# Differential attention on one core: score products with the second operand on 64 rows or on all 128

## The chip, the cores and the metric

The kernel runs on 1 core of one Trainium2 chip. The metric is the device time in microseconds of one execution. Three runs of the kernel before were timed.

## What is computed

A trunk of two decoder layers over 1024 tokens of width 1024, all in float32. Layer 0 mixes tokens by gated linear attention, layer 1 by differential attention; each mixer is followed by an MLP of width 4096 with a squared ReLU. The change lies in layer 1:

```python
def diff_mixer(h, cos, sin, w_in, lam_vecs, subln_g, w_o, lambda_init):
    H, dh, dv = DIFF_HEADS, DIFF_DH, DIFF_DV          # 8, 64, 128
    q, k, v = jnp.split(h @ w_in, 3, axis=-1)
    q = rope_partial(q.reshape(B, T, H, 2, dh), cos, sin) * (dh ** -0.5)
    k = rope_partial(k.reshape(B, T, H, 2, dh), cos, sin)
    ...
    for i in range(T // Q_BLOCK):                     # 8 query tiles of 128
        L = (i + 1) * Q_BLOCK
        s = jnp.einsum('bhiqd,bhikd->bhiqk', qb, k[:, :, :, :L]).astype(f32)
        p = jax.nn.softmax(jnp.where(mask, s, -jnp.inf), axis=-1)
        a = p[:, :, 0] - lam * p[:, :, 1]
        outs.append(jnp.einsum('bhqk,bhkv->bhqv', a.astype(v.dtype), v[:, :, :L]))
```

Each of the 8 heads has two softmaxes (s = 0, 1) with queries and keys of 64 dimensions of their own, and one set of values of 128 dimensions.

## The kernel before, in words

**Precision.** A float32 operand is cut into a rounded part hi and a rest lo = x - hi, both of type float32r. A product x·y is the sum hi·hi + hi·lo + lo·hi: three TensorE products (`mm3`, L115).

**Layer 1's order.** TensorE's instructions in this stage stand in an order written out by hand (L1054); those of ScalarE, VectorE and GpSimd are ordered by the framework's planner, and each engine works through its queue in order. Time is counted in slots. A slot issues one score block (L1062), the pieces that an `Agenda` has due (transpositions, values, norms), and between them pieces of the projections: three products of 384 columns each, 64 pieces to a head, about 2.67 pieces per slot. When the projections are through, pieces of the output projection (512 columns) take their place. The projections run ahead of the scores by 22 slots.

**Score blocks.** There are 192: for each head and softmax, query tile i (0 to 7) needs the keys 0 to 128(i+1). These come in blocks b of at most 512 columns: one block for i below 4 and two from i = 4 on. In the order of issue a head has 24 blocks: eight for tiles 0 to 3 (called its first part below), sixteen for tiles 4 to 7 (its second part). Block (i, s, b) is written as those three numbers. `scores` (L904) takes one of three PSUM buffers `ps_` and issues two products: L920 on all 128 rows, L921 on 64 rows. Then VectorE puts on the causal mask (L923) and takes the row maximum (L924); when the tile's last block has come, it makes the negative scaled maximum `nm`, and ScalarE takes the exponential (L936), which frees the buffer. After s = 1 VectorE forms the difference of the two softmaxes (L951).

**Operands of the scores.** `turn_qk` (L877) transposes rotated queries (gi = 0) or keys (gi = 2) of a head and a half of the tokens: 128 partitions, the 64 dimensions of s = 0 above those of s = 1. From that tile it makes, for each s:

- queries `q`: hi in the half of the partitions of s (ScalarE, L887), lo in the other half (VectorE, L889): [hi; lo];
- keys `kd`: hi in its own half (ScalarE, L896), copied to the other half by GpSimd (L900): [hi; hi]; and a tile `kl` with the lo parts of both s (VectorE, L898).

L920 multiplies [hi; lo] with [hi; hi]: hi·hi + lo·hi. L921 multiplies the hi half of the queries with the lo half of the keys, on 64 partitions: hi·lo.

**Behind the scores.** `turn_a` (L960) transposes the weights on TensorE (L966), ScalarE and VectorE cut them in two (L112, L113, tile `aT`), and `values` (L972) multiplies them with the values into `po`. `sub_rms` and `sub_norm` apply the head's norm. `rotate` (L863) is GpSimd's rotary embedding, six operations per head and half. In the last two heads VectorE and ScalarE also cut up the weights of the output projection and reloaded outputs (L1030), and add output products to x (L712).

Of the kernel before, what the change touches and what calls it, by code (L numbers as in the profile page):

```python
# [40 lines left out]

# How much other work of TensorE lies between a piece of work and one that needs its results: in
# rough microseconds of products (gated linear attention), in slots (differential attention).
GLA_LAG = dict(rank=1.09, decay=4.71, keys=3.36, score=4.04, out=7.24, step=2.16, turn=14.56, ada=30.5)
DIFF_LAG = dict(rotary=2.55, keys=1.95, turn=3, next=1.6, value=2, rms=2.66, norm=6.53)
DIFF_END = dict(turn=1.27, next=0.57, value=1.15, rms=1.1, norm=2)
DIFF_LEAD = 22
DIFF_RATE = {True: 2.0, False: 3.0}    # pieces of the output projection per slot, before and after its last operand


class Agenda:
    """Work that is put off until enough other work has been issued (`now` counts it)."""

# [16 lines left out]
def two_pi_parts():  # L70
    """2*pi cut into parts of four bits, so that a part times an integer below 2**20 is exact."""
    rest, parts = 2.0 * math.pi, []
    step = 2.0 ** -1
    while step > 2.0 ** -46:
        part = math.floor(rest / step) * step
        parts.append(part)
        rest -= part
        step /= 16.0
    return [p for p in parts if p]
# [3 lines left out]
def trunk(ctx: ExitStack, tc, a, out):  # L83
    nc = tc.nc
    pe, act, dve, pool = nc.tensor, nc.scalar, nc.vector, nc.gpsimd

# [1 line left out]
    const = ctx.enter_context(tc.tile_pool(name="const", bufs=1))  # L88
# [20 lines left out]

# [1 line left out]
    def split(hi, lo, src):  # L111
# [8 lines left out]
    def weight(src, shape, pinned=False):  # L120
        """Load a piece of a weight and split it into two parts of float32r."""
        raw = wraw.tile(shape, F32, name="raw", tag="raw")
        c0 = 0
        for part in src if isinstance(src, list) else [src]:
            c1 = c0 + part.shape[-1]
            i = nc.sync.dma_start(out=raw[:, :, c0:c1], in_=part)
            c0 = c1
            if pinned:
                in_order(i)
        hi = wsp.tile(shape, F32R, name="whi", tag="whi")  # L130
        lo = wsp.tile(shape, F32R, name="wlo", tag="wlo")
        split(hi, lo, raw)
        return hi, lo

    def wcols(w, c0, n, pinned=False):
        """Columns of a weight with its rows on partitions: [128, k, n]."""
        return weight(w.rearrange("(k p) n -> p k n", p=P)[:, :, c0:c0 + n], [P, KT, n], pinned)
# [9 lines left out]
    def rsqrt_cols(r, ms, scratch, n, scale=1.0 / D):  # L147
        """r = (ms * scale + eps) ** -0.5 for a few columns, with a Newton step."""
        m = scratch.tile([P, n], F32, name="rs_m", tag="rs_m")
# [9 lines left out]
    def broadcast(bc, cols, n):  # L159
        """bc[:, j*128:(j+1)*128] = cols[:, j] on every partition."""  # L160
        for j in range(n):
            pe.matmul(out=bc[:, j * P:(j + 1) * P], lhsT=cols[:, j:j + 1].broadcast_to([P, P]),  # L162
                      rhs=ident, start=True, stop=True)

    def norm_mod(x, half, h, gcols, shift, tmp, small, ps, cols=slice(0, HT), on_pool=()):
        """h = x / rms(x) * gcols + shift, in two parts, for the tokens cols of a half."""
        w = cols.stop - cols.start
# [30 lines left out]
    def ada_block(l, c0, n, raws, accs, ps, queue, tag="st", bufs=1):  # L198
        """mod[:, l, c0/128 ...] of n columns: products on VectorE, sum over partitions on PE."""
        ada_sums(l, c0, n, ada_products(l, c0, n, raws, accs, queue), ps, tag, bufs)  # L200
# [25 lines left out]
    def gscale(l, j):  # L226
        """norm_g * (1 + scale) of sub-layer j of layer l."""
        sc = mod[:, l, (3 * j + 1) * KT:(3 * j + 2) * KT]
        i = NG_ROW + (2 * l + j) * KT
        dve.scalar_tensor_tensor(out=gs[:, 2 * l + j, :], in0=sc, scalar=1.0, in1=colsT[:, i:i + KT],  # L230
                                 op0=ALU.add, op1=ALU.mult)
# [9 lines left out]

# [1 line left out]
    gla = ctx.enter_context(ExitStack())  # L243
# [123 lines left out]
    def log_sigmoid(z, bias, tp, tag1, tag2):  # L367
        """min(z + b, 0) and log(1 + exp(-|z + b|)); their difference in place of the first."""
        t1 = tp.tile([P, HT], F32, name="ls1", tag=tag1)
# [8 lines left out]
    with gla as g:  # L378
# [49 lines left out]
        def decays(u, first=False):  # L428
            """Cumulated decays of a head inside each tile of 128 tokens, around its middle."""
            hd = u["hd"]  # L430
# [53 lines left out]
        def out_step(u, j):  # L484
            """The outputs of a tile of 128 tokens, and the state behind it."""
            hd, half, v, qi, ks = (u[n] for n in ("hd", "half", "v", "qi", "ks"))
# [46 lines left out]
        def unit(hd, half, ws):  # L533
            """The projections of a head for half of the tokens, in pieces of three products."""
            u = dict(hd=hd, half=half, v=[])
# [90 lines left out]
        def stream():  # L626
            """The projections of all heads but the first unit's, and the first ones of the gates."""
            for hd in range(GLA_H):
# [46 lines left out]

# [1 line left out]
    def acc_mm():  # L677
        return mm.tile([P, HT], F32, name="acc", tag="mm")

    def out_proj(h, half, w_o, acc, done, ahead=False, ready=None):  # L680
        """The output projection of a mixer for half of the tokens, in pieces of three products; if
        it is ahead, the last tile of the rows comes at the end, on its own."""
        rows, ends = KT - 1 if ahead else KT, []
# [126 lines left out]

# [1 line left out]
    win = a["diff_w_in"][0]  # L812
    o = [[None, None] for _ in range(KT)]
    x = [[None, None] for _ in range(KT)]
    with ExitStack() as g:
# [12 lines left out]

        q, kd, kl, vs = ({} for _ in range(4))

        def projections():
            """The projections of all heads, in pieces of three products."""
            for hd in range(DIFF_H):
# [43 lines left out]
        def turn_qk(hd, half, qk, gi):  # L877
            """Queries as [hi; lo] and keys as [hi; hi] (and lo apart), with dimensions on partitions."""
            tr = dp.tile([P, HT], F32, name="tr", tag="tr", bufs=2)
# [3 lines left out]
            if gi == 0:  # L883
                t = [dv.tile([P, HT], F32R, name="q", tag=f"q{half}{i}", bufs=1) for i in range(2)]
                q[hd, half] = t
                for i in range(2):
                    act.copy(out=t[i][both[i]], in_=tr[both[i]])  # L887
                for i in range(2):
                    dve.tensor_tensor(out=t[i][both[1 - i]], in0=tr[both[i]], in1=t[i][both[i]].bitcast(F32),  # L889
                                      op=ALU.subtract)  # L890
            else:
                t = [dk.tile([P, HT], F32R, name="kd", tag=f"kd{half}{i}", bufs=2 - half) for i in range(2)]
                lo = dk.tile([P, HT], F32R, name="kl", tag=f"kl{half}", bufs=2 - half)
                kd[hd, half], kl[hd, half] = t, lo
                for i in range(2):
                    act.copy(out=t[i][both[i]], in_=tr[both[i]])  # L896
                for i in range(2):
                    dve.tensor_tensor(out=lo[both[i]], in0=tr[both[i]], in1=t[i][both[i]].bitcast(F32),  # L898
                                      op=ALU.subtract)
                    pool.tensor_copy(out=t[i][both[1 - i]], in_=t[i][both[i]])  # L900

        st_ = {}

        def scores(hd, i, s, b):  # L904
# [13 lines left out]
            qs = slice((i % 4) * P, (i % 4 + 1) * P)  # L918
            qt = q[hd, i // 4][s]
            pe.matmul(out=ps_[:, :w], lhsT=qt[:, qs], rhs=kd[hd, b][s][:, :w], start=True, stop=False)  # L920
            pe.matmul(out=ps_[:, :w], lhsT=qt[both[s], qs], rhs=kl[hd, b][both[s], :w], start=False, stop=True)  # L921
            if b == nb - 1:
# [37 lines left out]
        def turn_a(pair, j0):  # L960
            """Weights of two query tiles against two key tiles, with keys on partitions."""
            lastp = j0 == 2 * pair["pr"]
# [115 lines left out]
    def finish(half, cols, x, tp, sm, ps, acc_tile):  # L1078
        """The last norm with tokens on partitions, two tiles of tokens at a time."""
        if not grow:  # L1080
# [39 lines left out]
def diff_constants(tc, const, dc, pos, le, colsT):  # L1120
    """cos and sin of the rotary angles [128 tokens, 8 tiles, 8], -lambda, the sub-norm's gain and
    the causal mask (as an upper bound) of a diagonal block."""
    nc = tc.nc
# [64 lines left out]
```

## Time and profile before

| | us |
|---|---|
| median of 3 runs | 2598.0 |
| lowest and highest run | 2597.88, 2598.4 |
| span of the profiled execution | 2596.7 |
| TensorE busy | 2533.6 |
| VectorE busy | 1481.8 |
| ScalarE busy | 915.4 |
| GpSimd busy | 181.0 |

The profiled execution is one execution; its span goes from its first to its last instruction, 1.3 us less than the median of the runs. Engines are named PE (TensorE's products), PEld (TensorE's weight loads), DVE (VectorE), ACT (ScalarE) and POOL (GpSimd). L921 is line 921 of the kernel. Products on PE are pipelined: a product's shown duration overlaps with the next one's, so from the rows of the timeline the distance of starts is read. A row gives, for an instruction, start, duration, engine, line, operation, the tile written and the tiles read, its size (rows x columns of the weights, then partitions x columns that stream through), and in brackets the engine's idle time before it with what ended it.

### The profile page before, as it was taken

Reading aid. Unit: us, or ns where it says so; the run is one execution under the profiler, and the core shown is the slowest. Engines: PE = TensorE matmul, PEld = TensorE weight load, DVE = VectorE, ACT = ScalarE, POOL = GpSimd, SP = SyncE. Lnnn points to the kernel's source line nnn. Section 1 sums busy time; section 2 is a strip of 40 time slices with the busy share of each in tenths; the row PEclk is TensorE's granted clock in tenths of the full one; section 3 lists DMA queues with packets and bytes.
Section 4 is the critical chain, followed back from the end, with each engine's and each line's share of the span. In section 5 each row is a group of like instructions: output and inputs, shape, how many; then the busy total and the mean of one; then the engine's idle time right before and its main releaser. Section 6 shows DMA issues by size and latency. Waiting matters only on the chain.

```text
span 2596.7 us, 32374 instructions
## 1 busy us (share of the span) xinstructions
PE 2533.6 (98%) x12551; PEld 2114.2 (81%) x12551; DVE 1481.8 (57%) x2872; ACT 915.4 (35%) x1849; POOL 181.0 (7%) x322
## 2 busy tenths in 40 slices
PE   7899999999999999999999999999999999999998
PEld 5788878888888888888888888887788888888887
DVE  7877786745355445337677777687743343334334
ACT  5645555422112211224455554554422122212222
POOL 2111110001011001000211111110000000000000
PEclk9999999999999999999999999999999999999999
DMA  8333364213133223113001111023311111111111
GB/s 279 120 112 114 119 206 147 81 42 113 50 121 97 93 69 110 41 47 102 25 29 33 34 33 33 23 78 114 114 41 57 41 55 43 50 48 49 49 41 65
DMA packets 224025, 202.59 MB, mean 78 GB/s; under 512 B 10426, under 2 KB 194912, under 8 KB 223872
## 3 DMA queue, kind: packets, MB, share of 16 engines
q1 hardware_dynamic: 209472, 156.33, 19.5%
q0 software_dynamic: 12992, 41.97, 5.2%
q8 instruction: 98, 1.61, 0.3%
q10 hardware_dynamic: 1408, 2.24, 0.2%
q14 instruction: 55, 0.45, 0.1%
HBM read 180.57 MB, written 19.92 MB: 77 GB/s over the span
## 4 chain that ended last, share of the span: by engine, by line
PE 87%; issue 5%; DVE 3%; DMA 2%; ACT 2%; POOL 0%; DVEq 0%; SPq 0%; POOLq 0%; ACTq 0%
PE acc L116 20%; PE acc L117 20%; PE acc L118 20%; PE pp L116 5%; PE pp L118 3%; PE pp L117 3%; DMA ada_raw<-in_ada_w 2%; PE at L966 1%; PE bc L162 1%; PE pr L116 1%; PE pr L117 1%; PE pr L118 1%; PE po L117 1%; PE po L118 1%; PE po L116 1%
## 5 line engine op out<-in xcount | busy, mean ns | idle before, releaser
L116 PE MATMUL acc<-h_hi,whi 128*128 128x512 f32 x1280 | 505.0, 395 | 1.9 <-DVE x L712 1.8
L117 PE MATMUL acc<-h_lo,whi 128*128 128x512 f32 x1280 | 500.5, 391 | 0.0
L118 PE MATMUL acc<-h_hi,wlo 128*128 128x512 f32 x1280 | 500.4, 391 | 0.0
L112 ACT CAST whi<-raw 128x1024 fp32r<-128x1024 f32 (+2 forms) x217 | 221.1, 1020 | 714.3 <-PE acc L117 667.0
L712 DVE SCALAR_TENSOR_TENSOR x<-acc,mod,x 128x512 f32<-128x512 f32 (+1 forms) x312 | 224.2, 722 | 366.4 <-PE acc L118 365.7
L116 PE MATMUL acc<-hd,whi 128*128 128x512 f32 (+1 forms) x1088 | 412.9, 380 | 1.3 <-DVE x L712 1.3
L118 PE MATMUL acc<-hd,wlo 128*128 128x512 f32 (+1 forms) x1088 | 412.7, 379 | 0.0
L117 PE MATMUL acc<-hd,whi 128*128 128x512 f32 (+1 forms) x1088 | 412.3, 379 | 0.0
L113 DVE TENSOR_TENSOR wlo<-raw,whi 128x1024 fp32r<-128x1024 f32 (+2 forms) x217 | 258.5, 1192 | 132.7 <-ACT whi L112 125.7
L116 PEld LDWEIGHTS acc<-h_hi,whi 128*128 128x128 f32 x1280 | 240.9, 188 | 55.2 <-issue 3.6
L118 PEld LDWEIGHTS acc<-h_hi,wlo 128*128 128x128 f32 x1280 | 241.2, 188 | 50.3
L117 PEld LDWEIGHTS acc<-h_lo,whi 128*128 128x128 f32 x1280 | 241.2, 188 | 47.9
L116 PEld LDWEIGHTS acc<-hd,whi 128*128 128x128 f32 x1088 | 204.5, 188 | 42.5 <-DVE x L712 1.8
L118 PEld LDWEIGHTS acc<-hd,wlo 128*128 128x128 f32 x1088 | 204.4, 188 | 40.7
L117 PEld LDWEIGHTS acc<-hd,whi 128*128 128x128 f32 x1088 | 204.3, 188 | 40.7
L770 DVE TENSOR_TENSOR relu<-relu 128x512 f32<-128x512 f32 x128 | 88.0, 688 | 206.0 <-ACT relu L769 205.9
L116 PE MATMUL pp<-whi,h_hi 128*128 128x384 f32 x512 | 199.4, 389 | 0.0
L118 PE MATMUL pp<-whi,h_lo 128*128 128x384 f32 x512 | 172.9, 338 | 0.0
L117 PE MATMUL pp<-wlo,h_hi 128*128 128x384 f32 x512 | 172.5, 337 | 0.0
L769 ACT ACTIVATE relu<-acc 128x512 f32<-128x512 f32 x128 | 75.8, 593 | 219.9 <-PE acc L118 219.9
L207 POOL DMA_DIRECT2D ada_raw<-in_ada_w x160 | 85.9, 537 | 867.0 <-DVE ada_acc L210 531.9
L112 ACT CAST hd<-relu 128x512 fp32r<-128x512 f32 x128 | 79.4, 621 | 158.3 <-DVE relu L770 158.2
(1760 smaller groups left out, 3806.5 us busy)
## 6 DMA issues: line engine op xcount, KB each, us to landing
raw<-in_mlp_w SPq DMA_DIRECT2D x128, 512.0 KB, 3.6
ada_raw<-in_ada_w POOLq DMA_DIRECT2D x160, 256.0 KB, 3.3
raw<-in_gla_w_in SPq DMA_DIRECT2D x24, 512.0 KB, 4.0
raw<-in_diff_w_in SPq DMA_DIRECT2D x64, 192.0 KB, 2.9
raw<-in_diff_w_o SPq DMA_DIRECT2D x17, 512.0 KB, 3.7
aw<-in_ada_w SPq DMA_DIRECT2D x16, 512.0 KB, 7.6
raw<-in_gla_w_o SPq DMA_DIRECT2D x16, 512.0 KB, 3.9
x<-xs SPq DMA_DIRECT2D x32, 256.0 KB, 4.6
```

The lines of the kernel that those rows point to most:

```text
L112: act.copy(out=hi, in_=src)
L113: dve.tensor_tensor(out=lo, in0=src, in1=hi.bitcast(F32), op=ALU.subtract)
L116: pe.matmul(out=o, lhsT=lh, rhs=rh, start=start, stop=False)
L117: pe.matmul(out=o, lhsT=lh, rhs=rl, start=False, stop=False)
L118: return pe.matmul(out=o, lhsT=ll, rhs=rh, start=False, stop=stop)
L162: pe.matmul(out=bc[:, j * P:(j + 1) * P], lhsT=cols[:, j:j + 1].broadcast_to([P, P]), rhs=ident, start=True, stop=True)
L207: queue.dma_start(out=w, in_=a["ada_w"][l].rearrange("(k p) n -> p k n", p=P)[:, k:k + kk, c0:c0 + n])
L712: return dve.scalar_tensor_tensor(out=t, in0=psum, scalar=mcols(l, gate)[:, kt:kt + 1], in1=t, op0=ALU.mult, op1=ALU.add)
L769: act.activation(out=r, in_=pt, func=AF.Relu)
L770: dve.tensor_tensor(out=r, in0=r, in1=r, op=ALU.mult)
L966: pe.transpose(out=at[:, n * P:(n + 1) * P], in_=pair["es"][i][:, j * P:(j + 1) * P], identity=ident)
```

## The change

Queries are kept as two tiles for each s, [hi; hi] and [lo; lo], and keys as one tile [hi; lo]. Both score products of a block then use all 128 rows: [hi; hi]·[hi; lo] = hi·hi + hi·lo, and [lo; lo]·[hi; lo] = lo·hi + lo·lo. The term lo·lo, left out before, is now part of the sum. For the queries ScalarE writes the two hi parts, VectorE the two lo parts, each in its own half, and GpSimd copies all four to the other half. For the keys ScalarE writes hi and VectorE lo, and GpSimd does nothing. Per half of the tokens, four query tiles take the place of two, and two key tiles the place of three. Nothing else in the kernel's work changes.

```diff
         def turn_qk(hd, half, qk, gi):
 ...
             if gi == 0:
-                t = [dv.tile([P, HT], F32R, name="q", tag=f"q{half}{i}", bufs=1) for i in range(2)]
-                q[hd, half] = t
-                for i in range(2):
-                    act.copy(out=t[i][both[i]], in_=tr[both[i]])
-                for i in range(2):
-                    dve.tensor_tensor(out=t[i][both[1 - i]], in0=tr[both[i]], in1=t[i][both[i]].bitcast(F32),
-                                      op=ALU.subtract)
+                hi, lo = ([dv.tile([P, HT], F32R, name=f"q{n}", tag=f"q{n}{half}{i}", bufs=1) for i in range(2)]
+                          for n in "hl")
+                q[hd, half] = hi, lo
+                for i in range(2):
+                    act.copy(out=hi[i][both[i]], in_=tr[both[i]])
+                for i in range(2):
+                    dve.tensor_tensor(out=lo[i][both[i]], in0=tr[both[i]], in1=hi[i][both[i]].bitcast(F32),
+                                      op=ALU.subtract)
+                for t in (hi, lo):
+                    for i in range(2):
+                        pool.tensor_copy(out=t[i][both[1 - i]], in_=t[i][both[i]])
             else:
-                t = [dk.tile([P, HT], F32R, name="kd", tag=f"kd{half}{i}", bufs=2 - half) for i in range(2)]
-                lo = dk.tile([P, HT], F32R, name="kl", tag=f"kl{half}", bufs=2 - half)
-                kd[hd, half], kl[hd, half] = t, lo
+                t = [dk.tile([P, HT], F32R, name="k", tag=f"k{half}{i}", bufs=2 - half) for i in range(2)]
+                ks[hd, half] = t
                 for i in range(2):
                     act.copy(out=t[i][both[i]], in_=tr[both[i]])
                 for i in range(2):
-                    dve.tensor_tensor(out=lo[both[i]], in0=tr[both[i]], in1=t[i][both[i]].bitcast(F32),
+                    dve.tensor_tensor(out=t[i][both[1 - i]], in0=tr[both[i]], in1=t[i][both[i]].bitcast(F32),
                                       op=ALU.subtract)
-                    pool.tensor_copy(out=t[i][both[1 - i]], in_=t[i][both[i]])
 ...
         def scores(hd, i, s, b):
 ...
-            qt = q[hd, i // 4][s]
-            pe.matmul(out=ps_[:, :w], lhsT=qt[:, qs], rhs=kd[hd, b][s][:, :w], start=True, stop=False)
-            pe.matmul(out=ps_[:, :w], lhsT=qt[both[s], qs], rhs=kl[hd, b][both[s], :w], start=False, stop=True)
+            for n, qt in enumerate(q[hd, i // 4]):
+                pe.matmul(out=ps_[:, :w], lhsT=qt[s][:, qs], rhs=ks[hd, b][s][:, :w], start=n == 0, stop=n == 1)
```

## Rows read from the trace of the kernel before

**Rows 1.** The page: busy us, share of the span and instructions of each engine.
```profile
PE 2533.6 (98%) x12551; PEld 2114.2 (81%) x12551; DVE 1481.8 (57%) x2872; ACT 915.4 (35%) x1849; POOL 181.0 (7%) x322
```
**Rows 2.** Windows (stretch, length, busy by engine): head 3's parts, head 7's first.
```profile
core 0: us, PE busy (x) PEld busy (x) DVE busy (x) ACT busy (x) POOL busy (x), PEclk, DMA share, GB/s
1454.00:1477.00 23.00, 22.31 (x130) 19.01 (x128) 18.26 (x53) 12.71 (x31) 4.35 (x8) 1.00 0.27 81
1477.00:1523.00 46.00, 45.52 (x253) 38.02 (x254) 30.96 (x96) 21.92 (x65) 4.31 (x9) 1.00 0.02 7
1732.00:1756.00 24.00, 23.57 (x124) 18.27 (x122) 21.82 (x57) 15.90 (x37) 4.38 (x7) 1.00 0.37 111
```
**Rows 3.** Timeline of PE: blocks of 512, 384, 256 and 128 columns.
```profile
1517.93 0.40 PE L920 MATMUL ps__13513<-kd,q 128*128 128x512 f32 x1
1518.25 0.49 PE L921 MATMUL ps__13513<-kl,q 64*128 64x512 f32 x1
1518.67 0.44 PE L116 MATMUL pp<-whi,h_hi 128*128 128x384 f32 x1
1518.95 0.34 PE L117 MATMUL pp<-wlo,h_hi 128*128 128x384 f32 x1
1519.13 0.34 PE L118 MATMUL pp<-whi,h_lo 128*128 128x384 f32 x1
...
1502.22 0.34 PE L920 MATMUL ps__13335<-kd,q 128*128 128x384 f32 x1
...
1503.14 0.34 PE L117 MATMUL pp<-wlo,h_hi 128*128 128x384 f32 x1
...
1528.87 0.28 PE L920 MATMUL ps__13628<-kd,q 128*128 128x256 f32 x1
...
1529.67 0.33 PE L117 MATMUL pp<-wlo,h_hi 128*128 128x384 f32 x1
...
1523.63 0.22 PE L920 MATMUL ps__13572<-kd,q 128*128 128x128 f32 x1
...
1524.32 0.33 PE L117 MATMUL pp<-wlo,h_hi 128*128 128x384 f32 x1
```
**Rows 4.** Timeline of PEld: the weight loads around one block's second product.
```profile
1500.63 0.18 PEld L921 LDWEIGHTS ps__13325<-kl,q 64*128 64x128 f32 x1 [0.31 <-issue]
1501.06 0.19 PEld L116 LDWEIGHTS pp<-whi,h_hi 128*128 128x128 f32 x1 [0.25 <-issue]
```
**Rows 5.** Timeline of PE: products of 256 and 128 columns on 128 rows.
```profile
1526.85 0.28 PE L118 MATMUL po<-aT,v 128*128 128x256 f32 x1
1526.97 0.22 PE L116 MATMUL po<-aT,v 128*128 128x128 f32 x1
1527.03 0.28 PE L117 MATMUL po<-aT,v 128*128 128x128 f32 x1
1527.14 0.27 PE L118 MATMUL po<-aT,v 128*128 128x128 f32 x1
```
**Rows 6.** Windows of L921's instructions alone, over the whole stage.
```profile
1250.00:1810.00 560.00, 84.36 (x192) 35.24 (x192) 1.00 0.15 46
```
**Rows 7.** Groups by line on POOL, 1250 to 1760 us: busy, mean ns, idle before.
```profile
L900 POOL CAST kd<-kd 64x512 fp32r<-64x512 f32 x32 | 19.4, 607 | 171.9 <-issue 86.7 <-ACT kd L896 84.2
```
**Rows 8.** Timelines of DVE, PE and ACT: instructions that release or wait.
```profile
1402.30 1.39 DVE L889 TENSOR_TENSOR q<-tr,q 64x512 fp32r<-64x512 f32 x2
...
1407.94 0.50 PE L920 MATMUL ps__12264<-kd,q 128*128 128x512 f32 x1 [1.12 <-ACT et L936]
...
1520.27 0.69 ACT L936 ACTIVATE et<-ps__13459,nm 128x512 f32<-128x512 f32 x1
...
1521.10 0.50 PE L920 MATMUL ps__13537<-kd,q 128*128 128x512 f32 x1
...
1762.97 0.66 PE L116 MATMUL acc<-h_hi,whi 128*128 128x512 f32 x1 [1.57 <-DVE x L712]
```
**Rows 9.** Timeline of ACT: a cast of weights that stands for their transposition.
```profile
1519.89 0.48 ACT L112 CAST aT<-at 128x384 fp32r<-128x384 f32 x1 [4.86 <-PE at L966]
```

More of the change, by code (lines that the diff above doesn't have):

```diff
@@ L827, in lag @@
             return (DIFF_LAG if left else DIFF_END)[name]
-        q, kd, kl, vs = ({} for _ in range(4))
+        q, ks, vs = ({} for _ in range(3))
         def projections():
@@ L883, in turn_qk @@
             if gi == 0:
-                t = [dv.tile([P, HT], F32R, name="q", tag=f"q{half}{i}", bufs=1) for i in range(2)]
-                q[hd, half] = t
+                hi, lo = ([dv.tile([P, HT], F32R, name=f"q{n}", tag=f"q{n}{half}{i}", bufs=1) for i in range(2)]
[9 more added lines that the diff above has]
+                        pool.tensor_copy(out=t[i][both[1 - i]], in_=t[i][both[i]])
+            else:
+                t = [dk.tile([P, HT], F32R, name="k", tag=f"k{half}{i}", bufs=2 - half) for i in range(2)]
+                ks[hd, half] = t
                 for i in range(2):
@@ L890, in turn_qk @@
                                       op=ALU.subtract)
-            else:
-                t = [dk.tile([P, HT], F32R, name="kd", tag=f"kd{half}{i}", bufs=2 - half) for i in range(2)]
-                lo = dk.tile([P, HT], F32R, name="kl", tag=f"kl{half}", bufs=2 - half)
-                kd[hd, half], kl[hd, half] = t, lo
-                for i in range(2):
-                    act.copy(out=t[i][both[i]], in_=tr[both[i]])
-                for i in range(2):
-                    dve.tensor_tensor(out=lo[both[i]], in0=tr[both[i]], in1=t[i][both[i]].bitcast(F32),
-                                      op=ALU.subtract)
-                    pool.tensor_copy(out=t[i][both[1 - i]], in_=t[i][both[i]])
         st_ = {}
```

## The prediction

> **What bounds the kernel now.** I read the page first: TensorE is busy for 98% of the span, VectorE for 57% [rows 1]. So a change in a stage pays if it shortens TensorE's own stream there, and only as far as the other engines keep up in that stage. Next I cut the attention stage (about 1250 to 1810 us) by head. A head has 24 blocks of scores: eight for the query tiles 0 to 3 (one key half each) and sixteen for tiles 4 to 7 (two key halves). The windows show the two parts of head 3, and the first part of head 7 [rows 2]: TensorE fills 22.31 of 23.00 and 45.52 of 46.00 us, while VectorE has 18.26 (79%) and 30.96 (67%). Head 7 is the exception: VectorE is busy for 21.82 of 24.00 us there.
>
> Then I read TensorE's order of time around one block. Busy time is of no use for pipelined products; what counts is the step from one start to the next. A projection product of 384 columns steps by 0.17 to 0.18 us. Around a score block the steps are: first product 0.32, second product (on 64 rows) 0.42, and the projection product behind it 0.28 [rows 3], though that last one is the same product that takes 0.175 elsewhere. The weight loads say why [rows 4]: the 64-row load starts at the very moment at which its product is shown to start, after 0.31 us in which the loader did nothing, and the next full load again starts only with its own product, after 0.25 us. In the ordinary stream a load runs under the product before it. So both borders, from 128 rows to 64 and back, cost a hidden load its cover, and the pipeline runs empty there.
>
> **The change, part by part.**
>
> *Score products.* A block still has two products, of the same columns, with two weight loads; the second one now has 128 rows, so both borders go. From start of the first product to start of the second projection product behind the block, before [rows 3]: 512 columns 1518.95 - 1517.93 = 1.02 us, 384 columns 1503.14 - 1502.22 = 0.92, 256 columns 1529.67 - 1528.87 = 0.80, 128 columns 1524.32 - 1523.63 = 0.69. After, each product should take the step of a full-row product of its width: 0.12 for 256 columns and at most 0.11 for 128 [rows 5], 0.175 for 384 [rows 3], and for 512, one more step of 0.055, 0.23. With one projection product of 0.175 behind them that makes 0.635, 0.525, 0.415 and 0.395 us. The gain of a block is 0.385 for 512 columns, 0.395, 0.385 and 0.295 us; the steps of [rows 3] in the second decimal leave 0.01 to 0.02 open, and since the gain grows or holds with the width in the other three, I take 0.40 for 512.
>
> There are 192 blocks [rows 6]. By the loops a pair of head and softmax has 6 blocks of 512 columns and 2 each of 384, 256 and 128, and there are 16 pairs: 96 x 0.40 + 32 x 0.395 + 32 x 0.385 + 32 x 0.295 = 38.4 + 12.6 + 12.3 + 9.4 = **72.7 us** off TensorE's stream. The eight blocks of a head's first part carry 2 x (0.40 + 0.395 + 0.385 + 0.295) = 2.95 us of it.
>
> A rule weighed here: a 64-row load lasts 0.18 us, about what its neighbours last, so the load itself is not what gets shorter. The Trainium skill, "TensorE: Matmul & The Clock Gate", section on LDWEIGHTS, says that a load is priced by its columns and that one of 32 rows takes as long as one of 128; by that alone the sum would be nil. The Trainium skill, "TensorEngine Tiling (Array Packing)", Key Properties, says that a change of tiling mode drains TensorE; by that the sum stays 72.7. The steps of 0.42 and 0.28 decide for the second.
>
> *Queries and keys.* Keys: two ScalarE copies and two VectorE subtractions per half, as before, and the two GpSimd copies go. Queries: two copies and two subtractions as before, and four GpSimd copies come, of the form of the removed ones, 0.607 us each [rows 7]. Per head and half GpSimd has two more: 16 x 2 x 0.607 = 19.4 us, beside a GpSimd that is idle for most of the stage (busy for 4.35 of 23.00 us [rows 2]). On VectorE and ScalarE the work is the same, so I price it at nothing. What is new is the latency: a query tile is complete only when GpSimd has copied its two low parts. The tight case is the second half of a head's queries. Its subtractions end at 1402.30 + 1.39 = 1403.69 and the first score that reads it starts at 1407.94 [rows 8]: 4.25 us. The high copies can run while VectorE subtracts, so the last low copy ends some 0.6 us later, or 2.4 us later if all four run behind the subtractions. TensorE arrives three blocks, 1.2 us, sooner, which leaves 3.05. That cover hides either; without it the cost would be up to 2.4 us in each of 8 heads, 19 us. GpSimd's queue holds nothing else then but the rotation, whose next turn is half a head away. Keys become ready sooner, with one engine fewer in their chain.
>
> *What is late next.* (a) Head 7, first part: VectorE needs 21.82 us, and TensorE's 24.00 would become 21.05. VectorE is the bound, and TensorE already waits for it soon after, 1.57 us [rows 8]; I count the 2.95 us as lost. (b) In each of heads 0 to 6 the last block of tile 7 waits for its PSUM buffer: the exponential that frees it ends at 1520.96, and the block starts at 1521.10 [rows 8]. That exponential hangs on the block right before it in TensorE's order, the very block of 512 columns shown in [rows 3], whose second product and successor become 0.2 + 0.1 us shorter, so TensorE arrives 0.3 us too early: 7 x 0.3 = 2.1 us. (c) The wait of 1.12 us ahead of tile 4 (one in each of seven heads) [rows 8] hangs on a transposition of keys with no score product between; it stays, at no cost against before. (d) Waits that the trace doesn't show yet, as VectorE's share in a first part goes to 18.26 of 20.05, 91%: from nothing to the whole gain of the first parts of heads 0 to 6, 7 x 2.95 = 20.7 us. Below nothing, the order of VectorE's and ScalarE's queues is laid out anew, and the seven waits of (c), 7.8 us, could go. I take 5.5 us, nearer the low end, because VectorE is idle for a third of a second part [rows 2] and catches up there.
>
> *Sum.* 72.7 - 2.95 - 2.1 - 5.5 = 62.1 us. The profiled execution's span is 2596.7 us; 2596.7 - 62.1 = 2534.6. The median of the runs is 1.3 us above the span: **2536 us**.
>
> **The rivals.**
>
> *VectorE takes over.* All first parts lose their gain, 8 x 2.95 = 23.6 us, and (b) stays: 72.7 - 23.6 - 2.1 = 47.0, so 2551 us. For it: 91% busy in a first part, with a fixed order of queues, is what head 7 shows now, where TensorE falls behind. Against it: second parts are at 67%, and go to 78% only.
>
> *No gain.* The 64-row product may be dear for another reason than its rows, for instance since both products write one PSUM tile; then the steps stay and the time is 2598 us. For it: the load of 0.18 us, like any other. Against it: products on 128 rows that write one PSUM tile step by 0.12 and 0.11 us [rows 5], and it is the border back to 128 rows that costs 0.1 us in a product of another tile. The rule of the Trainium skill, "TensorE: Matmul & The Clock Gate", section on LDWEIGHTS, would lead here.
>
> *Slower: ScalarE's order.* Only TensorE's order is written by hand; the other queues are laid out anew. ScalarE stands 4.86 us for a transposition of TensorE's with exponentials queued behind it [rows 9], at present without harm. Its place would be the same turn of the weights in tiles 6 and 7; if the new order puts two exponentials that free score buffers behind such a wait in each head, TensorE stands for 8 x 2 x 4.86 = 77.8 us, less the 72.7 gained: 2603 us. It decides from 15 such waits on. Against it: the waits that now reach TensorE are 1.1 us, one in a head.
>
> **How the numbers follow.** The forecast case has 0.72, VectorE's takeover 0.22, no gain 0.03, slower 0.03. The measurement can tell about 0.2%, 5 us, from no change; the first two cases are faster by far more, so faster is 0.94, same 0.03, slower 0.03. The range: below, 72.7 with the waits of (c) gone, 2598.0 - 72.7 - 7.8 = 2517.5, of which I leave out the last corner: 2520. Above, the takeover, 2551, and half of the 19 us for late queries on it: 2561.
>
> **What would show it.** In the profile after: 192 second products on 128 rows, steps of 0.23 and 0.23 at 512 columns, the product behind a block at 0.175, and no loader gap of 0.25 to 0.3 us at a block. A head should take about 61 us instead of 69, VectorE's share should rise over 80%, GpSimd should have 64 copies of query parts and none of keys, and TensorE's waits for exponentials should be about 8 to 15 us in sum. Steps that stay at 0.42 would make it wrong, as would waits of over 25 us in the stage; a wait of a score product for GpSimd would show the query chain mispriced.

## The result, and the profile after

The changed kernel takes 2535.1 us (median of 4 runs, 2532.3 to 2536.8) against 2597.9 us (4 runs): a ratio of 0.9757, 95% interval 0.9743 to 0.9771, 62.8 us faster. The forecast was 2536 us, 62 us faster.

The page of the kernel after, busy time and instructions of each engine, beside [rows 1]:

```profile
PE 2464.6 (97%) x12551; PEld 2112.8 (83%) x12551; DVE 1478.5 (58%) x2872; ACT 914.5 (36%) x1849; POOL 202.3 (8%) x354
```

The number of products is the same; GpSimd has 32 instructions and 21 us more. The timeline of TensorE after, around two blocks of 512 columns of head 3 and one of 128 (L922 now issues both score products), beside [rows 3]:

```profile
1443.61 0.34 PE L118 MATMUL pp<-whi,h_lo 128*128 128x384 f32 x1
1443.78 0.39 PE L922 MATMUL ps__13018<-k,qh 128*128 128x512 f32 x1
1444.01 0.40 PE L922 MATMUL ps__13018<-k,ql 128*128 128x512 f32 x1
1444.24 0.34 PE L116 MATMUL pp<-whi,h_hi 128*128 128x384 f32 x1
1444.42 0.34 PE L117 MATMUL pp<-wlo,h_hi 128*128 128x384 f32 x1
...
1450.63 0.47 PE L922 MATMUL ps__13096<-k,qh 128*128 128x512 f32 x1 [1.20 <-ACT et L937]
...
1453.47 0.22 PE L922 MATMUL ps__13119<-k,qh 128*128 128x128 f32 x1
1453.53 0.27 PE L922 MATMUL ps__13119<-k,ql 128*128 128x128 f32 x1
1453.63 0.39 PE L116 MATMUL pp<-whi,h_hi 128*128 128x384 f32 x1
1453.87 0.34 PE L117 MATMUL pp<-wlo,h_hi 128*128 128x384 f32 x1
```

At 512 columns the steps are 0.23, 0.23 and 0.18 us, 0.64 in sum instead of 1.02. The loads of the same block, beside [rows 4]:

```profile
1443.61 0.19 PEld L922 LDWEIGHTS ps__13018<-k,qh 128*128 128x128 f32 x1
1443.78 0.19 PEld L922 LDWEIGHTS ps__13018<-k,ql 128*128 128x128 f32 x1
1444.01 0.19 PEld L116 LDWEIGHTS pp<-whi,h_hi 128*128 128x128 f32 x1
```

Each load starts a whole step ahead of its product (1443.78 for the product at 1444.01), and the loader's gaps are gone. The windows after, on head 3's two parts and head 7's first, beside [rows 2]:

```profile
core 0: us, PE busy (x) PEld busy (x) DVE busy (x) ACT busy (x) POOL busy (x), PEclk, DMA share, GB/s
1430.00:1450.00 20.00, 19.43 (x130) 18.80 (x129) 17.95 (x53) 12.48 (x31) 6.13 (x10) 1.00 0.31 92
1450.00:1490.00 40.00, 39.28 (x252) 37.84 (x253) 30.45 (x96) 21.58 (x65) 5.08 (x10) 1.00 0.02 8
1675.00:1698.00 23.00, 20.19 (x118) 17.12 (x118) 21.55 (x55) 16.12 (x37) 6.92 (x10) 1.00 0.37 115
```

The same work of head 3 fits into 60 us instead of 69, with VectorE at 90% and 76%; head 7's first part has VectorE at 94% and TensorE no longer full.

Over all 192 blocks the medians, from the start of the first product to that of the second projection product behind, are:

| columns | blocks | before, us | after, us | gain, us |
|---|---|---|---|---|
| 512 | 96 | 1.038 | 0.647 | 0.391 |
| 384 | 32 | 0.917 | 0.526 | 0.391 |
| 256 | 32 | 0.800 | 0.413 | 0.387 |
| 128 | 32 | 0.689 | 0.399 | 0.290 |

96 x 0.391 + 32 x (0.391 + 0.387 + 0.290) = 71.7 us. That is 9.0 us for each head, and this is what the heads got, from the start of a head's first score product to that of the next head's (head 7: to its last block):

| head | 0 | 1 to 5, each | 6 | 7 | sum |
|---|---|---|---|---|---|
| before, us | 60.3 | 69.5 | 70.0 | 75.3 | 553.1 |
| after, us | 53.1 | 60.6 | 62.6 | 70.5 | 489.4 |
| gain, us | 7.2 | 8.9 | 7.4 | 4.7 | 63.7 |

So 8 of the 71.7 us don't arrive, and nearly all of them are missing at the two ends of the stage: 1.8 in head 0, 1.6 in head 6, 4.2 in head 7.

### The profile page after: what moved, and what is told of

It reads as the page before. It is cut to its first block, busy times and chain, and to the rows that moved or that the text cites. A ratio compares the mean times of both kernels' runs of the same rounds, so it can differ in the third digit from the quotient of the medians.

```text
span 2534.9 us, 32430 instructions
## 1 busy us (share of the span) xinstructions
PE 2464.6 (97%) x12551; PEld 2112.8 (83%) x12551; DVE 1478.5 (58%) x2872; ACT 914.5 (36%) x1849; POOL 202.3 (8%) x354
## 4 chain that ended last, share of the span: by engine, by line
PE 44%; DVE 3%; ACT 2%; DMA 2%; issue 1%; DVEq 0%; POOL 0%; ACTq 0%; SPq 0%; POOLq 0%
PE acc L116 10%; PE acc L117 9%; PE acc L118 9%; PE pp L116 3%; PE pp L118 3%; PE pp L117 3%; PE at L967 1%; DMA raw<-in_diff_w_o 1%; PE po L117 1%; PE po L118 1%; PE bc L162 1%; PE po L116 1%; ACT et L937 1%; PE tr L881 0%; PE st L998 0%
## 5 line engine op out<-in xcount | busy, mean ns | idle before, releaser
L118 PE MATMUL acc<-h_hi,wlo 128*128 128x512 f32 x1280 | 500.0, 391 | 0.0
L118 PE MATMUL acc<-hd,wlo 128*128 128x512 f32 (+1 forms) x1088 | 412.3, 379 | 0.0
L118 PEld LDWEIGHTS acc<-h_hi,wlo 128*128 128x128 f32 x1280 | 241.0, 188 | 50.5
L118 PEld LDWEIGHTS acc<-hd,wlo 128*128 128x128 f32 x1088 | 204.3, 188 | 40.9
L116 PE MATMUL pp<-whi,h_hi 128*128 128x384 f32 x512 | 182.8, 357 | 0.0
L118 PE MATMUL pp<-whi,h_lo 128*128 128x384 f32 x512 | 172.7, 337 | 0.0
```

The source lines that it names most:

```text
L116: pe.matmul(out=o, lhsT=lh, rhs=rh, start=start, stop=False)
L118: return pe.matmul(out=o, lhsT=ll, rhs=rh, start=False, stop=stop)
```

## The experiments

Each run is compared with runs of the kernel before on the same chip; ratios are to that, and a difference between two variants of the changed kernel is taken from their ratios.

**Undoing the rows alone.** In the changed kernel:

```diff
-            for n, qt in enumerate(q[hd, i // 4]):
-                pe.matmul(out=ps_[:, :w], lhsT=qt[s][:, qs], rhs=ks[hd, b][s][:, :w], start=n == 0, stop=n == 1)
+            qh, ql = q[hd, i // 4]
+            pe.matmul(out=ps_[:, :w], lhsT=qh[s][:, qs], rhs=ks[hd, b][s][:, :w], start=True, stop=False)
+            pe.matmul(out=ps_[:, :w], lhsT=ql[s][both[s], qs], rhs=ks[hd, b][s][both[s], :w], start=False, stop=True)
```

> The changed kernel with all its operands and copies, but its second score product again on the 64 rows that hold lo of the queries and hi of the keys (the term lo*lo is left out, as in the kernel before). Theory, the borders between 128-row and 64-row products cost the time: the whole gain goes back, 2597 us (2590 to 2604), and at 512 columns the steps of starts are again 0.33, 0.43 and 0.28 us. Rival, the new operands bring the gain (keys without GpSimd, one tile fewer): it stays at 2535 us (2530 to 2541).

Measured: 2599.2 us, ratio 1.0009 (1.0000 to 1.0019). The whole gain is gone. TensorE's timeline of this run, a block of 512 columns:

```profile
1515.92 0.40 PE L922 MATMUL ps__13540<-k,qh 128*128 128x512 f32 x1
1516.25 0.49 PE L923 MATMUL ps__13540<-k,ql 64*128 64x512 f32 x1
1516.67 0.44 PE L116 MATMUL pp<-whi,h_hi 128*128 128x384 f32 x1
1516.95 0.34 PE L117 MATMUL pp<-wlo,h_hi 128*128 128x384 f32 x1
```

The steps of 0.33, 0.42 and 0.28 us are back, with the new operands in place.

**Doing the rows alone.** In the kernel before:

```diff
-            pe.matmul(out=ps_[:, :w], lhsT=qt[both[s], qs], rhs=kl[hd, b][both[s], :w], start=False, stop=True)
+            pe.matmul(out=ps_[:, :w], lhsT=qt[:, qs], rhs=kl[hd, b][:, :w], start=False, stop=True)
```

> The kernel before with its operands and copies, but its second score product on all 128 rows of [hi; lo] and of the tile with both softmaxes' lo keys: beside hi*lo it adds the product of lo queries with the other softmax's lo keys, which doesn't belong there. Theory of the borders: the whole gain without the new operands, 2535 us (2528 to 2543), steps of 0.23, 0.23 and 0.18 us. Rival, new operands: no change, 2597 us (2590 to 2604).

Measured: 2531.9 us, ratio 0.9753 (0.9737 to 0.9769). Its timeline of TensorE:

```profile
1445.44 0.39 PE L920 MATMUL ps__12991<-kd,q 128*128 128x512 f32 x1
1445.67 0.40 PE L921 MATMUL ps__12991<-kl,q 128*128 128x512 f32 x1
1445.91 0.34 PE L116 MATMUL pp<-whi,h_hi 128*128 128x384 f32 x1
1446.09 0.34 PE L117 MATMUL pp<-wlo,h_hi 128*128 128x384 f32 x1
```

One line gives all of the gain. The new operands neither bring nor cost anything that the measurement can tell; they are what makes full rows come out as the right sum.

**Border or product.** In the kernel before, the first product too on 64 rows, the same ones as the second:

```diff
-            pe.matmul(out=ps_[:, :w], lhsT=qt[:, qs], rhs=kd[hd, b][s][:, :w], start=True, stop=False)
+            pe.matmul(out=ps_[:, :w], lhsT=qt[both[s], qs], rhs=kd[hd, b][s][both[s], :w], start=True, stop=False)
```

> The kernel before with its first score product on 64 rows as well, the same rows as the second (the term lo*hi is left out). Theory of the borders: two borders to a block as before, one ahead of the first and one behind the second product, none between: the step between the two products falls to 0.23 us at 512 columns, the sum of the block's steps stays near 1.04 us, and the time is 2598 us (2588 to 2608). Rival, every 64-row product pays for its own uncovered load: some 0.2 us more in each of 192 blocks, 2636 us (2620 to 2660). Rival, the cost lies between the two products of one PSUM tile: no difference from before in the step between them.

Measured: 2595.4 us, ratio 0.9999 (0.9990 to 1.0009), so twice as many 64-row products cost the same. TensorE's products and then its weight loads in this run:

```profile
1515.44 0.34 PE L118 MATMUL pp<-whi,h_lo 128*128 128x384 f32 x1
1515.70 0.49 PE L920 MATMUL ps__13513<-kd,q 64*128 64x512 f32 x1
1516.04 0.39 PE L921 MATMUL ps__13513<-kl,q 64*128 64x512 f32 x1
1516.36 0.45 PE L116 MATMUL pp<-whi,h_hi 128*128 128x384 f32 x1
1516.65 0.34 PE L117 MATMUL pp<-wlo,h_hi 128*128 128x384 f32 x1
```

```profile
1515.70 0.18 PEld L920 LDWEIGHTS ps__13513<-kd,q 64*128 64x128 f32 x1 [0.25 <-issue]
1515.81 0.19 PEld L921 LDWEIGHTS ps__13513<-kl,q 64*128 64x128 f32 x1
1516.36 0.19 PEld L116 LDWEIGHTS pp<-whi,h_hi 128*128 128x128 f32 x1 [0.36 <-issue]
```

The 64-row load of L921 starts at 1515.81, 0.23 us ahead of its product at 1516.04: behind another 64-row product it is hidden like any load. The two loads that stand in the open are the first of each kind. The expected step of 0.23 between the two products missed, though: it is 0.34. A product whose load is in the open is shown from the start of that load, so a border is spread over two steps. Behind L118 the step is 0.26 instead of 0.175, and behind L920 0.34 instead of 0.23; then 0.32 instead of 0.23, and 0.29 instead of 0.175. By these steps a border is a pause of about 0.09 us and about 0.11 that the open load adds (its row lasts 0.18 to 0.19), 0.2 us in all, 0.39 to 0.4 for the two of a block in either kernel. That is the 0.391 of the table. The sign that was named for a cost between two products of one PSUM tile, no difference in their step, is what came (0.34, and 0.32 before). It doesn't speak for that rival: in the run before this one two products of one tile step by 0.23, and here the step holds the open load of L920.

**The copies on GpSimd.** In the changed kernel every copy of the queries twice:

```diff
                     for i in range(2):
-                        pool.tensor_copy(out=t[i][both[1 - i]], in_=t[i][both[i]])
+                        for _ in range(2):
+                            pool.tensor_copy(out=t[i][both[1 - i]], in_=t[i][both[i]])
```

> The changed kernel with each GpSimd copy of the queries made twice: eight copies of 0.62 us for a head and half instead of four. Theory, the copies lie beside other work: within 3 us of the changed kernel, though the last copy comes up to 2.5 us later, since a score needs the queries some 4 us after the subtractions. Rival, the copies are on the path: up to 2.5 us in each of 16 turns, 20 to 40 us slower.

Measured beside a second timing of the changed kernel itself: 2534.2 us, ratio 0.9765 (0.9752 to 0.9779), against 0.9761 (0.9748 to 0.9775), for which the text on record was:

> The changed kernel itself, as the measure for the other runs beside it: 0.976 of the kernel before, 2533 us (2529 to 2538).

So 80 us of copies on GpSimd (groups by line of the doubled run: L895 ql x64, 40.8 us, and qh x63, 39.7 us) cost no more than 40 do, as far as the measurement can tell. They lie beside other work.

**VectorE's subtractions of the reloaded outputs, on GpSimd.**

```diff
-                    split(t[0], t[1], raw)
+                    act.copy(out=t[0], in_=raw)
+                    pool.tensor_tensor(out=t[1], in0=raw, in1=t[0].bitcast(F32), op=ALU.subtract)
```

> The changed kernel with the twelve subtractions that cut up the reloaded outputs (128x512, 0.69 us each on VectorE, all within heads 6 and 7) moved to GpSimd. Theory, VectorE's load is what keeps heads 6 and 7 from their full gain (they got 12.2 of 18.5 us): 3 us faster than the changed kernel (1 to 6), the first part of head 7 about 21.5 us instead of 23.2. Rival, these heads wait for something else: no difference.

Measured: 2542.2 us, ratio 0.9797 (0.9784 to 0.9811): 9 us slower than the changed kernel, not 3 faster. VectorE in head 7's first part went from 93% to 76%, and the part took 25.5 us instead of 23.2; head 6 went from 62.6 to 68.5. Timelines of ScalarE, VectorE, TensorE and GpSimd in this run:

```profile
1658.98 1.04 ACT L112 CAST whi<-raw 128x1024 fp32r<-128x1024 f32 x1 [4.34 <-DMA raw<-in_diff_w_o]
...
1660.06 1.22 DVE L113 TENSOR_TENSOR wlo<-raw,whi 128x1024 fp32r<-128x1024 f32 x1 [2.40 <-ACT whi L112]
...
1663.96 1.09 PE L967 MATMUL at<-ident,et 128*128 128x128 f32 x4 [4.66 <-DVE ql L890]
...
1653.68 1.29 POOL L1032 TENSOR_TENSOR h_lo<-raw,h_hi 128x512 fp32r<-128x512 f32 x1
```

A subtraction takes 1.29 us on GpSimd, and this one ends at 1654.97. The reload and the weights of the output projection share two raw buffers, and the load of weights into the buffer that it lets go is issued at 1655.00. ScalarE stands 4.34 us for that load, the copies of queries stand behind that cast in its queue, VectorE's subtraction of the queries behind both, and TensorE 4.66 us for VectorE. The window of the stretch from late in that wait on:

```profile
1662.10:1668.90 6.80, 4.93 (x19) 4.87 (x20) 4.39 (x12) 2.43 (x7) 1.55 (x3) 0.50 0.27 77
```

The granted clock, third number from the end, is 0.50 here: that is the lower of TensorE's two levels, 1.2 GHz, and it fell while the engine stood still. Projection products in this stretch step by 0.32 us instead of 0.175, so the wait costs head 6 some of the clock beside its own 4.66 us.

**The reload left out.** I formed the theory that those two buffers hold up heads 6 and 7 in the changed kernel too. In head 7 its chain that ended last, in order of time (start, us, what), leaves TensorE for two loads of some 4 us:

```profile
1677.13 3.97 DMA raw<-in_diff_w_o
...
1686.19 0.61 DVE aT L113
1686.85 0.39 PE po L117
...
1697.08 4.08 DMA raw<-in_diff_w_o
```

```diff
-                    raw = wraw.tile([P, HT], F32, name="raw", tag="raw")
-                    nc.sync.dma_start(out=raw, in_=os_[k, :, half * HT:(half + 1) * HT])
-                    split(t[0], t[1], raw)
+                    split(*(u.rearrange("p (j c) -> p j c", c=P) for u in t), ident.unsqueeze(1).broadcast_to([P, 4, P]))
```

> The changed kernel without the reload of the outputs of heads 0 to 5: their two parts are made from the identity matrix, which lies in SBUF, so the output projection gets that in place of these heads' outputs. ScalarE's and VectorE's work is the same; twelve loads of 256 KB and their use of the two raw buffers are gone. Theory, heads 6 and 7 are held up by loads of weights that wait for a raw buffer: 4 us faster than the changed kernel (2 to 7), the two loads of 4 us drop out of the chain that ended last. Rival, VectorE's load holds them up: no difference (within 2 us).

Measured: 2535.2 us, ratio 0.9761 (0.9748 to 0.9775), no difference; the theory falls as to the whole. Of the two loads one is still in the chain. Head 6 gained 1.2 us (61.4), head 7 lost 2 (72.6). The same chain in this run, TensorE's row at its end, and the window that follows (columns as in the windows above):

```profile
1678.71 3.88 DMA raw<-in_diff_w_o
...
1686.48 4.21 DVE h_lo L113 x6
1690.68 0.61 DVE aT L113
...
1691.34 0.56 PE L117 MATMUL po<-aT,v 128*128 128x256 f32 x1 [3.90 <-DVE aT L113]
...
1691.40:1694.80 3.40, 3.40 (x13) 3.00 (x14) 1.44 (x8) 0.56 (x2) 0.00 (x0) 0.50 0.00 0
```

With no loads to pace them the six subtractions stand in a row on VectorE, 4.21 us, and TensorE waits 3.90 us for the weights behind them; then the granted clock is 0.50 (1.2 GHz) from 1691.40 to 1694.80. Both are costs that this run brings with it, so for head 7 it doesn't decide the theory; head 6 did wait for the loads, by 1.2 us.

**The mask left out.**

```diff
-            if b == nb - 1:
-                dve.tensor_tensor(out=ps_[:, w - P:w], in0=ps_[:, w - P:w], in1=cmin, op=ALU.min)
```

> The changed kernel without the causal mask of the diagonal blocks (VectorE's minimum, 128 of them, 0.29 us each, 37 us in sum). If VectorE at 88 to 93% in the heads' first parts costs time, the heads get shorter: by up to 2 us in each of heads 0, 6 and 7, and 10 us in sum if heads 1 to 5 are bound by it as well. If TensorE's stream is the bound in heads 1 to 5, these stay at 20.5 and 40.2 us, and the whole is 2 to 5 us faster.

Measured: 2527.4 us, ratio 0.9733 (0.9719 to 0.9746), some 7 us faster than the changed kernel. The windows of this run, head 3's parts and head 7's first:

```profile
1427.00:1447.00 20.00, 19.33 (x128) 18.44 (x126) 16.11 (x42) 11.98 (x31) 5.15 (x10) 1.00 0.31 92
1448.00:1487.00 39.00, 38.94 (x252) 37.48 (x251) 27.94 (x85) 20.72 (x63) 5.08 (x10) 1.00 0.02 8
1672.00:1695.00 23.00, 20.70 (x123) 17.64 (x121) 20.40 (x50) 16.22 (x37) 7.14 (x10) 1.00 0.36 115
```

Head 3 keeps its length (61.0 us), with VectorE down from 90% to 80%: heads 1 to 5 are bound by TensorE's stream. Head 7 falls from 70.5 to 66.4 us, of which 0.5 us lies in its first part, and head 0 from 53.1 to 52.0; head 6 is at 63.2. Some of head 7's fall is the clock: in the profile of the changed kernel above the granted clock is 0.51 from 1705.80 to 1709.20, in head 7's second part; its other profile and this run have no such stretch in head 7, and there the fall is from 69.3 to 66.4. In the profiles the stage is 3 to 4 us shorter than in the changed kernel's two; the rest of the 7 us lies outside the stage, where the code is the same. There the other ten profiles spread over some 8 us, and this one lies 4 us below the lowest of them. That part stays open.

**The keys a slot earlier.** `DIFF_LAG`'s keys 0.95 instead of 1.95, in the changed kernel.

> The changed kernel with the keys' turn one slot earlier (keys lag 0.95 instead of 1.95). Theory, the wait of 1.2 us ahead of tile 4 comes from exponentials queued on ScalarE behind the keys' copies, which stand for a transposition just issued: with the transposition a slot earlier the seven waits shrink or go, 2528 us (2525 to 2532). Rival, the wait is ScalarE's work itself: it stays, 2533 us.

Measured: 2551.2 us, ratio 0.9832 (0.9819 to 0.9846): 18 us slower. The waits ahead of tile 4 did go, from 1.2 to 0.1 us each, as the theory said. But waits of TensorE in this run (total us, times, longest):

```profile
PE tr L881 <- DVE ql L890: 6.4, 7, 1.1
PE bc L162 <- DVE k L901: 5.1, 6, 2.0
```

and, in its timeline, the last block of tile 7 in each of six heads:

```profile
1434.34 0.50 PE L922 MATMUL ps__12750<-k,qh 128*128 128x512 f32 x1 [0.85 <-ACT et L937]
```

The keys' transposition now follows the queries' by one slot, and both go through the two PSUM buffers that `at`, `st` and `bc` share; and the planner ordered the other engines' queues anew. A wait of 1.2 us in a head was given up for about 3.

## Why the prediction was right, point by point

- **Score products, 72.7 us.** Right: 71.7. The gain was 0.391, 0.391, 0.387 and 0.290 us against 0.40, 0.395, 0.385 and 0.295. The cause is shown, not only argued: rows alone give and take the whole, and only borders cost. The rule of the Trainium skill, "TensorE: Matmul & The Clock Gate", section on LDWEIGHTS, holds for a load's duration (0.18 us on 64 rows, 0.19 on 128). The time lost here is not in that duration but in the gap ahead of the load and in its lost cover. "TensorEngine Tiling (Array Packing)", Key Properties, in the Trainium skill names the drain at a change of mode; the third run agrees and puts 0.2 us on it, load included.
- **GpSimd's copies, nothing.** Right. After, the subtractions of head 3's second query half end at 1447.43 and the last copy at 1448.17, 0.74 us later (0.6 was forecast), and the first score that reads it starts at 1450.63, held by an exponential.
- **(a) Head 7's first part, 2.95 lost.** 2.2 were lost (24.0 to 23.2 us). That VectorE's work alone sets the length of this part is not shown. The run without the mask took 1.6 us of VectorE's work out of it, and the part got 0.5 us shorter; in the run with subtractions on GpSimd VectorE went to 76%, and the part got 2.2 us longer. What held it there stays open.
- **(b) Tile 7's last block, 2.1 lost.** Wrong. TensorE's step into that block is 0.34 to 0.37 us before and after, in heads 1 to 5. The prediction misread what the exponential hangs on: it frees the buffer of the tile's first block (7, 0, 0), and in ScalarE's queue it stands right behind the cast of weights of [rows 9], which waits for a transposition on TensorE (L966 before, L967 after the change). Head 3 before:

```profile
1519.31 0.49 PE L966 MATMUL at<-ident,et 128*128 128x128 f32 x3
```

and after:

```profile
1486.83 0.49 PE L967 MATMUL at<-ident,et 128*128 128x128 f32 x3
1487.41 0.48 ACT L112 CAST aT<-at 128x384 fp32r<-128x384 f32 x1 [4.07 <-PE at L967]
1487.82 0.69 ACT L937 ACTIVATE et<-ps__13486,nm 128x512 f32<-128x512 f32 x1
...
1488.65 0.50 PE L922 MATMUL ps__13564<-k,qh 128*128 128x512 f32 x1
```

  The block starts 0.14 us behind the end of that exponential in both kernels. From the transposition to the block it is 1.79 us before and 1.82 after, and no score product lies between them. So the shortened products come ahead of both, as in (c), and nothing is lost. The cast's wait was not "without harm" either, as the prediction had it: the exponential behind it holds TensorE here, by some 0.2 us a head (the products of 256 columns ahead of the block step by 0.12).
- **(c) The wait ahead of tile 4 stays.** Right: 1.12 before, 1.20 after. TensorE's waits for exponentials in the stage come to 8.5 us in sum, at the low end of the 8 to 15 named as a sign.
- **(d) 5.5 lost elsewhere in heads 0 to 6.** 3.8 were: 1.8 in head 0, 1.6 in head 6, 0.4 in heads 1 to 5 together. They are not where the prediction put them, in first parts with VectorE at 91%: in heads 1 to 6 a first part went from 23.3 to 20.5 us, nearly the whole of its 2.9. In head 0 a score product now waits 0.7 us for VectorE's part of the keys; in head 6 the run without the reload got 1.2 us back. Not counted at all were 2 us in head 7's second part (51.3 to 47.3 us, against 6.0 at the prices of the table). The low clock doesn't explain them, since both profiles have such a stretch there (1763.2 to 1766.6 before, behind a wait of 1.57 us; 1705.8 to 1709.2 after, behind one of 1.97). Their cause stays open.

The losses come to 8 us, forecast 10.6, against a gain 1 us smaller than forecast; outside the stage the profile after is 2 us longer, within the spread there. That the sum lies within 1 us of the median is partly the luck of errors that cancel. VectorE's takeover, the likeliest rival, would have shown in heads 1 to 5; at 90% in a first part VectorE took next to nothing from them (0.4 us in five heads).

## What to carry to other kernels

Look for products on fewer rows that stand alone between full ones: the price is not in their rows but in the two borders, 0.4 us together here (0.3 at 128 columns), and it is read from steps of starts and from gaps of the weight loader. Filling the unused rows with something harmless or useful saves it, and such products next to each other share the two borders. And a stage in which several engines hand work around in a fixed order need not answer to a lighter load on one of them: read what stands behind the moved instruction in its new queue, and which buffers it keeps.

## What was not expected

With both products of a block on 64 rows the step between them stayed at 0.34 us, where 0.23 was expected, though the time stayed as expected. Moving one transposition by one slot cost 18 us, over a quarter of the whole gain, while it removed the very wait that it was meant to. And 8.3 us of VectorE's work taken to an engine that was mostly idle made the kernel 9 us slower, in head 6 by way of two raw buffers.
